# Low halves of the projection weights of tiles 3 to 7: GpSimd in the place of the vector engine

## The chip, the cores and the metric

The kernel runs on one core of a Trainium2 chip. The metric is the device time of one launch in microseconds (us). A core has five engines that run side by side, each with its own instruction queue: PE (TensorE, matrix products), DVE (the vector engine), ACT (ScalarE), POOL (GpSimd) and SP (SyncE, which here issues DMA transfers). SBUF is the on-chip memory that all of them read; PSUM is where PE puts its results.

## The reference

One layer of a decoder with 512 tokens and a model width of 1024. What matters here is the start: x is normalised, scaled and shifted by vectors that come from a condition c, and multiplied with a projection matrix. The rest (two groups of attention heads, gates, output projection) follows on its results.

```python
mod = jax.nn.silu(c) @ w_ada + b_ada
shift, scale, gate = jnp.split(mod, 3, axis=-1)
h = rms_norm(x, norm_gain) * (1 + scale[:, None, :]) + shift[:, None, :]
proj = h @ w_in
(q_a, k_a, v_a, z_a, q_b, kc, vc, ks, vs, kw, vw, z_b, g_b) = jnp.split(proj, _split_points(), axis=-1)
...
out = y.astype(x.dtype) @ w_out
return x + gate[:, None, :] * out
```

## The kernel before, in words

**Two halves for precision.** PE multiplies in a reduced float type, fp32r. To keep accuracy, every operand is split: the high half is the value copied into fp32r, the low half is the value minus its high half. A product of h and w is then three products: high h with high w, high h with low w, low h with high w.

**Phase one** makes the first 768 columns of the projection (q_a, k_a, v_a). The width of 1024 is cut into eight tiles of 128 rows, k = 0 to 7. For each tile:
- SP loads two transfers of rows of `w_ada` (`load_ada`, L232) and one piece of the projection weights, 128 x 768 (`load_wst`, L236). The staging tiles of both are rings of four (`ada_ring`, `wst_ring`), so the load for tile k + 4 waits for those who read tile k.
- DVE makes scale and shift of the tile with two row products over 1024 columns (`mod_rows`, L245; both inputs in SBUF), which leave one number per row in `AB`. For the first two tiles PE does this.
- DVE scales x by the norm (`scaled`, L296: `xT` from SBUF times `rbp` from PSUM).
- ACT makes `hh`, the high half of h, and `hf`, all of h (`h_high`, L302). DVE makes `hl`, the low half (`h_low`, L305; both inputs in SBUF).
- ACT makes the high half of the weights (`weights_high`, L288), and DVE the low half (`weights_low`, L291: `wst` minus the high half, both in SBUF). The halves lie in a ring of three pairs, named `sw0h`, `sw0l` to `sw2h`, `sw2l`; tile k uses pair k modulo 3.
- PE then runs `first_proj(k, n)` (L312, L313) for n = 0, 1, 2: high h with high w, high h with low w, low h with high w, each over four blocks of 128 tokens.

**The order** of this phase is written out by hand: all instructions are chained on each engine in the order in which they stand in the program (`in_order`). In the loop over k, `first_proj(k, 0)` and `first_proj(k, 1)` come first, then `new_tile(k + 1)`, then `first_proj(k, 2)`. `new_tile(k)` issues: `h_high(k)` on ACT; the first row product of tile k + 1 on DVE; `h_low(k)`; the second row product of tile k + 1; a scaling; the high half of the weights of tile k + 1 on ACT, and its low half on DVE. The scaling in it is that of tile k + 2 for k below 3, that of tile k + 1 for k from 4 to 6, and none for k = 3. So on DVE the low half of the weights of tile k + 1 is the last instruction of `new_tile(k)`, and the row products of the next `new_tile` stand behind it.

When phase one ends, ACT reads the sums from PSUM, and PE goes on with the next piece of the projection, whose weights are loaded through the `raw` tiles (`load_next`, L174) and split by `split` (ACT L192, DVE L193). GpSimd does little in the whole kernel: some memsets at the start, tiny copies of 128 x 2 in the attention (L1028), and a few transfers at the end.

Of the kernel before, what the change touches and what calls it, by code (L numbers as in the profile page):

```python
# [9 lines left out]
F32 = mybir.dt.float32  # L10
# [4 lines left out]
OP = mybir.AluOpType  # L15
# [18 lines left out]
NR = 4  # L34
LW = 4
PE_MODS = 2
GATE = {4: "kn2", 6: "qn11", 7: "qn11"}


# [36 lines left out]
@contextmanager  # L76
def in_order(tc, after=(), only=None):

    traced = tc.nc.cur_bb.bb.instructions
    n = len(traced)  # L80
    last = dict(after)
    yield last
    info = mybir.DependencyInfo(mybir.DependencyClass.NoSync, mybir.DependencyReason.DATA)
    for i in tc.nc.cur_bb.bb.instructions[n:]:
        if only and i.engine not in only:
            continue
        if i.engine in last:
            tc.add_manual_dep(i, last[i.engine].name, info, reason="in_order")
        last[i.engine] = i
# [3 lines left out]
def hybrid_layer_kernel(ctx, tc, A, out):  # L93
    nc = tc.nc
    PE, DVE, ACT, POOL, SP = nc.tensor, nc.vector, nc.scalar, nc.gpsimd, nc.sync
# [119 lines left out]
    ada, wst = {}, {}  # L215
# [5 lines left out]
    def load_ada(k):  # L221
        t = ada_ring[:, k % NR]
        if k < PE_MODS:
            ada[k] = t.rearrange("p (a b c) -> p a b c", a=8, b=2)
# [4 lines left out]
        else:  # L229
            ada[k] = t.rearrange("p (a b) -> p a b", a=2)  # L230
            for e in range(2):
                SP.dma_start(ada[k][:, e], A["w_ada_rows"][k - PE_MODS][:, e])  # L232

# [33 lines left out]
    hf, y, ws = {}, {}, {}  # L267
# [20 lines left out]
        ACT.activation(ws[k][0], wst[k], AF.Copy)  # L288

    def weights_low(k):  # L290
        DVE.tensor_tensor(ws[k][1], wst[k], ws[k][0].bitcast(F32), op=OP.subtract)  # L291

    def scaled(k, by, parts=(slice(0, S),)):
        y[k] = xT[k]
# [21 lines left out]
    with in_order(tc) as begun:  # L316
# [97 lines left out]
        ACT.copy(lsb[0:40, LINE - NEAR:LINE], pl)  # L414
        ACT.activation(hf[0], y[0], AF.Identity, bias=AB[:, 0, 1:2], scale=AB[:, 0, 0:1])
        weights_low(0)
        scaled(1, rbp)
        scaled(2, rbp)
# [3 lines left out]
        def new_tile(k):  # L422

            if k == 4:
                ACT.preload_act_table_set("exp_and_others")
            h_high(k, halves if k < 4 else (slice(0, S),))
            if k < 7:
                mod_rows(k + 1, (1 if k == 1 else 0,))
            h_low(k)
            if 1 < k < 7:  # L430
                mod_rows(k + 1, (1,))
            if k < 3:
                scaled(k + 2, rbp)
            if 4 <= k < 7:
                scaled(k + 1, rbp)
            if k < 7:
                weights_high(k + 1)
                weights_low(k + 1)

        for k in range(8):  # L440
            if k + NR < 8:
                load_ada(k + NR)
                load_wst(k + NR)
            elif k == LW:
                for _ in range(5):
                    load_next()
            first_proj(k, 0)
            if k == 0:
                mod_pe(1)
                weights_high(1)  # L450
                first_proj(0, 1, (0, 1))
                mod_col(1)
                mod_ab(1)
                weights_low(1)
                first_proj(0, 1, (2, 3))
            else:
                first_proj(k, 1)
            if k < 7:
                new_tile(k + 1)
            if k == 0:  # L460
                ACT.copy(lsb[0:8, LINE - NEAR - 128:LINE - NEAR], lsb[0:8, LINE - NEAR:LINE - NEAR + 128])
                ACT.copy(lsb[32:40, 0:LINE - NEAR], lsb[32:40, LINE - NEAR:LINE - NEAR + 1].to_broadcast([8, LINE - NEAR]))
                for a in range(2):
                    SP.dma_start(line_d[a], lsb[32 * a:32 * a + 8, :])
            if k >= 6:
                split_to("kv_cmp", 2 * (k - 6) + 1, 0)
            first_proj(k, 2)
# [291 lines left out]
    def gate_slice(q):  # L759

        for h in range(2):
            n, w = 2 * q + h, raws[f"gate{q}", h]
            with in_order(tc, {DVE.engine: marks[GATE[n]]} if n in GATE else {}, (DVE.engine,)):
                DVE.tensor_tensor_reduce(out=w, in0=w, in1=scrow, scale=0.5, scalar=prm[:, 16 + n:17 + n],
# [500 lines left out]
    with in_order(tc, last, (DVE.engine, ACT.engine)):  # L1265
# [3 lines left out]
        with in_order(tc, {PE.engine: last_pe()}, (PE.engine,)):  # L1269
            for name in TAIL.split():  # L1270
                op, rest = name[0], name[1:]
# [3 lines left out]
def _layout(inp):  # L1275
# [5 lines left out]
    halves = lambda t: cc(t.reshape(t.shape[0], 2, 4, t.shape[2]).transpose(1, 0, 2, 3))  # L1281
    wa = g("w_ada")[0].reshape(8, 128, 3, 8, 128)[:, :, 0:2, 0:PE_MODS]
    a["w_ada_cols"] = cc(wa.reshape(4, 2, 128, 2, PE_MODS, 128).transpose(4, 0, 2, 1, 3, 5).reshape(PE_MODS, 4, 128, 512))
    wr = g("w_ada")[0].reshape(D, 3, 8, 128)
    a["w_ada_rows"] = cc(wr[:, 0:2, PE_MODS:].transpose(2, 3, 1, 0))
    for q in range(4):
# [64 lines left out]
```

## Time and profile before

| | us |
|---|---|
| median of 3 runs | 299.51 |
| lowest and highest of these | 299.44, 300.15 |
| the profiled execution, its own time | 299.99 |
| its span in the trace | 297.7 |
| busy: PE, DVE, ACT, POOL | 290.1, 261.0, 205.1, 9.6 |
| first matmul of tile 3 and of tile 7 | 29.33, 46.99 |
| the low half of the weights on DVE (L291), one | 0.95 |

The span runs from the first to the last instruction in the trace; the time of the execution has some 2.3 us around it. Rows of a timeline show the start in us from the span's start, the length in us, the engine, the line, the operation, the tiles written and read, and in brackets how long the engine stood idle before it and what ended that. An instruction of DVE may start a little before the one in front of it has ended, so that the step from start to start is shorter than the length.

### The profile page before, as it was taken

To read this page: it belongs to the slowest core of one execution; us is meant where nothing else is said; L and a number is where in the kernel's file an instruction comes from. 1 tells how busy PE (TensorE), PEld (TensorE's weight loads), DVE (VectorE), ACT (ScalarE), POOL (GpSimd) and SP (SyncE) were. 2 spreads that over 40 slices of the span, in tenths; PEclk is the share of its full clock that TensorE was granted. 3 is DMA by queue.
4 is the path that set the end of the run, shared out by engine and by line. 5 is a ranking of instruction groups with operands and counts; after the bars stand their busy time and mean duration, and the time that the engine had idled before them with its cause. 6 is when DMAs were issued, how large, how long until landed. Compare 5 with 4: busy or idle time off the path is not lost.

```text
span 297.7 us, 6067 instructions
## 1 busy us (share of the span) xinstructions
PE 290.1 (97%) x2181; PEld 254.6 (86%) x2182; DVE 261.0 (88%) x730; ACT 205.1 (69%) x501; POOL 9.6 (3%) x28
## 2 busy tenths in 40 slices
PE   7999999999999999999999999999999999999995
PEld 3678888789989989989878988888888888889995
DVE  3689998999995998998999999999979779599992
ACT  5778657777848574967858567878877869567510
POOL 1000000000000100000000000000000000021210
PEclk9999999999999999999999999999999999999999
DMA  7999987842485884361402440223100120027272
GB/s 246 388 405 380 356 309 226 299 161 70 140 275 156 238 266 132 109 211 37 135 11 71 140 133 10 71 73 143 44 28 2 61 83 2 0 44 188 53 160 89
DMA packets 27417, 44.27 MB, mean 149 GB/s; under 512 B 1867, under 2 KB 18412, under 8 KB 27388
## 3 DMA queue, kind: packets, MB, share of 16 engines
q1 hardware_dynamic: 26380, 42.49, 42.2%
q0 software_dynamic: 864, 1.31, 3.0%
q8 instruction: 17, 0.28, 0.4%
q10 hardware_dynamic: 144, 0.09, 0.1%
q14 instruction: 12, 0.10, 0.1%
HBM read 41.74 MB, written 2.14 MB: 147 GB/s over the span
## 4 chain that ended last, share of the span: by engine, by line
PE 70%; DVE 13%; DMA 10%; ACT 3%; issue 2%; SPq 0%; DVEq 0%; ACTq 0%
PE pj L528 16%; PE pj L518 11%; PE po L1095 8%; PE pj L1205 6%; PE s L1004 5%; PE pt L1076 4%; DMA wst_ring<-in_w_qkv_a 4%; DMA ada_ring<-in_w_ada_rows 4%; PE s L1205 3%; PE pt L1062 3%; PE s L657 2%; DVE wl L193 2%; PE po L528 2%; DVE ada_ring L245 2%; PE s L1019 2%
## 5 line engine op out<-in xcount | busy, mean ns | idle before, releaser
L518 PE MATMUL pj<-wh,hh 128*128 128x256 f32 (+1 forms) x128 | 37.2, 291 | 0.0
L518 PE MATMUL pj<-wh,hl 128*128 128x256 f32 (+1 forms) x128 | 36.9, 288 | 0.0
L518 PE MATMUL pj<-wl,hh 128*128 128x256 f32 (+1 forms) x128 | 36.7, 287 | 0.0
L1010 ACT ACTIVATE pp<-pp,nm 128x256 f32<-128x256 f32 (+2 forms) x48 | 29.2, 610 | 6.3 <-DVE nm L1006 5.7
L528 PE MATMUL pj<-hh,wh 128*128 128x512 f32 x72 | 28.9, 402 | 0.0
L528 PE MATMUL pj<-hl,wh 128*128 128x512 f32 x72 | 28.8, 400 | 0.0
L528 PE MATMUL pj<-hh,wl 128*128 128x512 f32 x72 | 28.7, 399 | 0.0
L192 ACT ACTIVATE wh<-raw 128x512 fp32r<-128x512 f32 (+1 forms) x40 | 24.7, 635 | 5.3 <-PE pj L528 3.8
L193 DVE TENSOR_TENSOR wl<-raw,wh 128x512 fp32r<-128x512 f32 (+1 forms) x40 | 27.1, 692 | 1.4 <-ACT wh L192 1.1
L1006 DVE CUSTOM_DVE_ANT_0 pp<-s,bias 128x256 f32<-128x256 f32 (+2 forms) x48 | 25.5, 550 | 2.2 <-PE s L1004 2.0
L518 PEld LDWEIGHTS pj<-wh,hh 128*128 128x128 f32 x128 | 24.1, 189 | 0.4 <-issue 0.3
L518 PEld LDWEIGHTS pj<-wh,hl 128*128 128x128 f32 x128 | 24.2, 189 | 0.2 <-issue 0.2
L518 PEld LDWEIGHTS pj<-wl,hh 128*128 128x128 f32 x128 | 24.2, 189 | 0.1
L1004 PE MATMUL s<-kTb,qs 128*128 128x256 f32 (+2 forms) x96 | 23.6, 348 | 0.0
L1047 DVE TENSOR_SCALAR pp<-pp,rr,grev 128x256 f32<-128x256 f32 (+2 forms) x48 | 21.2, 474 | 0.3
L1004 PEld LDWEIGHTS s<-kTb,qs 128*128 128x128 f32 x96 | 16.9, 189 | 3.1 <-DVE nm L1006 0.3
L1010 ACT ACTIVATE pa<-pa,nm 128x129 f32<-128x129 f32 x32 | 12.7, 398 | 7.7 <-DVE nm L1026 6.0
L1077 ACT COPY ptT<-pt 128x384 f32<-128x384 f32 (+1 forms) x32 | 15.6, 526 | 1.1 <-PE pt L1076 1.0
L1063 ACT COPY ptT<-pt 128x256 f32<-128x256 f32 (+1 forms) x28 | 12.8, 457 | 4.1 <-PE pt L1062 3.7
L528 PEld LDWEIGHTS pj<-hh,wl 128*128 128x128 f32 x72 | 13.6, 188 | 2.4
L528 PEld LDWEIGHTS pj<-hl,wh 128*128 128x128 f32 x72 | 13.6, 189 | 2.3
L1076 PE MATMUL pt<-first,pp 128*128 128x128 f32 x112 | 15.5, 275 | 0.0
(320 smaller groups left out, 830.6 us busy)
## 6 DMA issues: line engine op xcount, KB each, us to landing
ada_ring<-in_w_ada_rows SPq DMA_DIRECT2D x12, 512.0 KB, 7.5
raw<-in_w_cmp SPq DMA_DIRECT2D x8, 512.0 KB, 6.6
raw<-in_w_gate SPq DMA_DIRECT2D x8, 512.0 KB, 4.5
raw<-in_w_o SPq DMA_DIRECT2D x8, 512.0 KB, 3.2
wst_ring<-in_w_qkv_a SPq DMA_DIRECT2D x8, 384.0 KB, 7.9
bias<-line_d SPq DMA_DIRECT2D x12, 256.0 KB, 4.0
xTp<-in_xT SPq DMA_DIRECT2D x8, 256.0 KB, 3.8
raw<-in_w_q_b SPq DMA_DIRECT2D x4, 512.0 KB, 4.8
```

What stands on the lines that cost most here:

```text
L192: ACT.activation(wh, src, AF.Copy)
L193: DVE.tensor_tensor(wl, src, wh.bitcast(F32), op=OP.subtract)
L518: PE.matmul(bank[:, t * n:(t + 1) * n], h[:, tb * 128:(tb + 1) * 128], w[:, k % 2, :], start=k == 0 and m == 0, stop=k == 7 and m == 2)
L528: PE.matmul(bank, w, h, start=k == 0 and m == 0, stop=k == 7 and m == 2)
L1004: PE.matmul(ps, qs[8 + 4 * g + r][:, 128 * i:128 * i + 128], kT[br, g][:, hl_, 0:w], start=hl_ == 0, stop=hl_ == 1)
L1006: DVE.tensor_tensor_reduce(out=P[:, g, 0:w], in0=ps, in1=bias["b", r, g][:, 512 - w:512], scale=1.0, scalar=3e38, op0=OP.add, op1=OP.min, ...
L1010: ACT.activation(P[:, g], P[:, g], AF.Exp, bias=nm[:, g:g + 1], scale=-1.0, accum_out=dn[:, g:g + 1])
L1047: DVE.tensor_scalar(v, v, rr[:, g:g + 1], gates[:, g, br:br + 1], op0=OP.mult, op1=OP.mult)
L1076: PE.transpose(pt[:, b * 128:(b + 1) * 128], P[:, g, b * 128:(b + 1) * 128], ident)
L1077: ACT.copy(T[:, 0:nb, :], rev(pt[:, 0:nb * 128].rearrange("p (b q) -> p b q", b=nb)))
L1095: PE.matmul(o[64 * g:64 * g + 64, 128 * i:128 * i + 128], vb[:, 64 * g:64 * g + 64], sl["T"][g][:, b, :], start=first_of and b == 0, stop= ...
L1205: PE.matmul(parts[g, p], a[:, r, :], b, start=new and r == 0 and m == 0, stop=r == 3 and m == 2, skip_group_check=True)
```

## The change

`weights_low` issues its subtraction on GpSimd for tiles 3 to 7 and on the vector engine for tiles 0 to 2. Operands, result, place in the program and the waits that follow from the data are the same. On GpSimd too the instructions of phase one are chained in program order.

```diff
 PE_MODS = 2
+POOL_LOWS = 3
 GATE = {4: "kn2", 6: "qn11", 7: "qn11"}
...
     def weights_low(k):
-        DVE.tensor_tensor(ws[k][1], wst[k], ws[k][0].bitcast(F32), op=OP.subtract)
+        (DVE if k < POOL_LOWS else POOL).tensor_tensor(ws[k][1], wst[k], ws[k][0].bitcast(F32), op=OP.subtract)
```

## The prediction

> **What bounds the kernel now.** I read the page's first part, then the stretches of the first phase by engine, then the timelines of DVE and ACT inside it. The page first:
>
> ```profile
> span 297.7 us, 6067 instructions
> PE 290.1 (97%) x2181; PEld 254.6 (86%) x2182; DVE 261.0 (88%) x730; ACT 205.1 (69%) x501; POOL 9.6 (3%) x28
> ```
>
> PE is busy for 290.1 of 297.7 us, so over the whole kernel it has 7.6 us idle: whatever makes PE late anywhere has little slack to vanish in later, and whatever makes it early can win little. GpSimd (POOL) is nearly empty. The change lies wholly in the first phase, the projection of eight weight tiles. This table has one row for each of tiles 2 to 6, from the first matmul of the tile to the first of the next (columns: stretch and its length, then busy time and instruction count of PE, PEld, DVE, ACT, POOL, then clock, DMA share, GB/s):
>
> ```profile
> 25.12:29.33 4.21, 4.21 (x26) 3.68 (x25) 3.85 (x8) 2.92 (x7) 0.00 (x0) 1.00 1.03 383
> 29.33:33.70 4.37, 4.37 (x27) 3.58 (x25) 4.37 (x7) 3.46 (x5) 0.00 (x0) 1.00 1.00 338
> 33.70:38.01 4.31, 4.31 (x26) 3.79 (x25) 4.16 (x8) 2.48 (x4) 0.00 (x0) 1.00 1.00 382
> 38.01:42.44 4.43, 4.37 (x26) 3.56 (x24) 4.43 (x8) 2.26 (x4) 0.00 (x0) 1.00 0.84 319
> 42.44:46.99 4.55, 4.46 (x25) 3.68 (x25) 4.45 (x7) 2.27 (x4) 0.00 (x0) 1.00 0.44 130
> ```
>
> Tile 2 takes 4.21 us with no gap: that is PE's own pace. The following four take 4.37, 4.31, 4.43 and 4.55, and DVE is full for nearly the whole of tiles 3, 5 and 6. So DVE limits this phase, but by little: from tile 4's start at 33.70, three tiles at PE's pace would bring tile 7 to 33.70 + 3 x 4.21 = 46.33 instead of 46.99. **0.66 us is all that freeing DVE can win here.** Why DVE is full, and how PE hangs on it, shows in the two timelines (start, length, engine, line):
>
> ```profile
> 32.07 0.96 DVE L291 TENSOR_TENSOR sw1l<-wst_ring,sw1h 128x768 fp32r<-128x768 f32 x1
> 32.94 1.28 DVE L245 CUSTOM_DVE_ANT_0 ada_ring<-ada_ring,scrow,first 128x1024 f32<-128x1024 f32 x1
> 34.14 0.09 DVE L245 DVE_READ_ACCUMULATOR2_ANT AB<- 128x1 f32 x1
> 34.38 0.69 DVE L305 TENSOR_TENSOR hl<-hf,hh 128x512 fp32r<-128x512 f32 x1 [0.15 <-ACT hf L302]
> 34.99 1.34 DVE L245 CUSTOM_DVE_ANT_0 ada_ring<-ada_ring,scrow,prmg 128x1024 f32<-128x1024 f32 x1
> 36.26 0.08 DVE L245 DVE_READ_ACCUMULATOR2_ANT AB<- 128x1 f32 x1
> 36.26 0.68 DVE L296 TENSOR_TENSOR xTp<-xTp,pj 128x512 f32<-128x512 f32 x1
> 36.86 0.95 DVE L291 TENSOR_TENSOR sw2l<-wst_ring,sw2h 128x768 fp32r<-128x768 f32 x1
> 37.73 1.28 DVE L245 CUSTOM_DVE_ANT_0 ada_ring<-ada_ring,scrow,first 128x1024 f32<-128x1024 f32 x1
> 38.93 0.08 DVE L245 DVE_READ_ACCUMULATOR2_ANT AB<- 128x1 f32 x1
> 38.93 0.68 DVE L305 TENSOR_TENSOR hl<-hf,hh 128x512 fp32r<-128x512 f32 x1
> 39.53 1.33 DVE L245 CUSTOM_DVE_ANT_0 ada_ring<-ada_ring,scrow,prmg 128x1024 f32<-128x1024 f32 x1
> 40.80 0.08 DVE L245 DVE_READ_ACCUMULATOR2_ANT AB<- 128x1 f32 x1
> 40.80 0.68 DVE L296 TENSOR_TENSOR xTp<-xTp,pj 128x512 f32<-128x512 f32 x1
> 41.40 0.95 DVE L291 TENSOR_TENSOR sw0l<-wst_ring,sw0h 128x768 fp32r<-128x768 f32 x1
> 42.27 1.28 DVE L245 CUSTOM_DVE_ANT_0 ada_ring<-ada_ring,scrow,first 128x1024 f32<-128x1024 f32 x1
> ...
> 45.34 0.68 DVE L296 TENSOR_TENSOR xTp<-xTp,pj 128x512 f32<-128x512 f32 x1
> ```
>
> ```profile
> 25.56 0.85 ACT L288 ACTIVATE sw0h<-wst_ring 128x768 fp32r<-128x768 f32 x1
> ...
> 39.77 0.85 ACT L288 ACTIVATE sw0h<-wst_ring 128x768 fp32r<-128x768 f32 x1 [1.22 <-DMA wst_ring<-in_w_qkv_a]
> ...
> 46.12 0.82 ACT L302 ACTIVATE hh<-xTp,AB 128x512 fp32r<-128x512 f32 x1 [2.28 <-DVE xTp L296]
> ```
>
> Per tile DVE does one row product (L245), the low half of h (L305), the second row product, the scaling of x (L296) and, last, the low half of the weights (L291), which the change moves. Starts follow each other faster than the lengths say, so I price by the step from one start to the next: low half of weights 0.87 (36.86 to 37.73), first row product 1.20, low half of h 0.60, second row product 1.27, scaling 0.60. The last scaling, at 45.34, releases ACT's high half hh at 46.12, and tile 7 starts on PE when that ends (46.12 + 0.82 = 46.94, start 46.99). So the scalings decide when tiles start, and the low half of the weights matters only as something that stands in front of the next scaling.
>
> **The change, part by part.** DVE loses five instructions, those of tiles 3 to 7, at 0.87 each: 4.35 us of DVE time. The one of tile 7 comes after the last scaling, so four can move a scaling. POOL gains the same five. No memory, transfer or order on the other engines changes.
>
> The price on POOL: the trace of before has no two-input instruction there. The nearest rows:
>
> ```profile
> 0.74 0.20 POOL L136 MEMSET ones_sq<- 128x128 f32 x1 [0.29 <-POOLq L1341]
> 0.88 0.41 POOL L321 MEMSET raw<- 8x384 f32 x1
> ```
>
> ```profile
> 98.81 0.65 POOL L1028 COPY pa<-nsink 128x2 f32<-128x2 f32 x1 [6.24 <-DVE csh L667]
> 101.39 0.19 POOL L1028 COPY pa<-nsink 128x2 f32<-128x2 f32 x1 [1.93 <-PE pt L1062]
> ```
>
> From 128 to 384 columns a memset grows by 0.21 us, 0.82 ns a column; one pass over 768 columns is 0.63. A tiny copy costs 0.19, which I take as the fixed part. If the two reads and the write run side by side, the instruction takes 0.19 + 0.63 = 0.82; if the two reads go in turn, 1.45; if the write goes in turn too, 2.08. DVE's 0.95 for the same shape shows no more than that 0.82 is fast. I take the middle of the two serial cases, **P = 1.76 us**, and keep 0.82 to 2.08. The Trainium skill (GPSIMD Engine Reference, section 3.1 Elementwise) gives 4497 ns for a two-input f32 add over 2048 columns; scaled to 768 columns that is an estimate of 1.69 us, no run here shows it, and the sum below would be +1.25 us by it.
>
> Whether POOL's work lies *beside* DVE's is the real question, and the copy of 0.65 us speaks to it. Beside it on DVE ran
>
> ```profile
> 98.74 0.68 DVE L571 TENSOR_TENSOR qn<-qraw,n_a 128x512 f32<-128x512 f32 x1
> ```
>
> with both inputs in SBUF. That instruction ended at 98.74 + 0.68 = 99.42, and the copy, begun at 98.81, ended at 99.46, 0.46 longer than the undisturbed one. I read this as a POOL read that could not go on until the two-input DVE instruction was through. The Trainium skill (SBUF — State Buffer, section Who interferes with whom) says that a DVE instruction with two SBUF inputs and a GpSimd instruction that reads SBUF contend for one read interface, and that the second to come is fully blocked; the trace agrees for a POOL copy behind DVE (0.65 against 0.19), and no row of before shows the other direction. On DVE the two row products and the low half of h have both inputs in SBUF; the scaling has one in PSUM (pj). I assume that the exclusion holds both ways and that POOL holds the interface for all of P. I also assume that POOL gets in only where DVE has no two-input instruction ready, since such instructions follow each other without a gap (the row product at 37.73 begins before 36.86 + 0.95 = 37.81).
>
> ```profile
> 27.52 0.68 DVE L296 TENSOR_TENSOR xTp<-xTp,pj 128x512 f32<-128x512 f32 x1
> 28.12 0.95 DVE L291 TENSOR_TENSOR sw0l<-wst_ring,sw0h 128x768 fp32r<-128x768 f32 x1
> 28.99 1.28 DVE L245 CUSTOM_DVE_ANT_0 ada_ring<-ada_ring,scrow,first 128x1024 f32<-128x1024 f32 x1
> ```
>
> The replay with P = 1.76, each DVE instruction at its step:
> - Tile 3's weights are ready at 25.56 + 0.85 = 26.41. POOL gets in beside the scaling, 27.52 to 29.28; the row product, free at 28.12, waits until 29.28 instead of starting at 28.99: **+0.29**, which is P - 0.60 - 0.87 (held, less the scaling beside it, less the instruction removed).
> - Tile 4: no scaling follows in that round. The row product of 32.94 now starts at 32.94 + 0.29 - 0.87 = 32.36 and ends at 33.57. DVE then must wait for ACT's hf (the row of 34.38), POOL gets in, and holds until 35.33. So the low half of h starts at 35.33 instead of 34.38: **+0.95**, with tile 3's 0.29 in it. The weights are late by 0.23 as well, since PE wants them a third into the tile, 33.70 + 1.40 = 35.10; that is covered, as tile 5 waits longer for its scaling.
> - Tiles 5 and 6: POOL beside the scalings, at 37.20 and 42.04, and the same +0.29 each. DVE is now behind its old times by 0.95 + 0.29 + 0.29 = **1.53**: the scaling of 45.34 comes at 46.87, hh at 47.65, and PE starts tile 7 at 48.52.
> - Tile 7's own low half runs from 46.87 to 48.63, before PE needs it at 48.52 + 1.40 = 49.92: nothing.
>
> In general the sum is 3(P - 1.47) + (P - 1.10) (three rounds beside a scaling, and tile 4's): +0.29 at P = 1.45, +1.53 at 1.76, +2.81 at 2.08. It crosses zero at 1.38 and 0.9 us at 1.60.
>
> What moves beside it costs nothing. The load of tile 7's weights goes into the staging slot of tile 3 and now waits for POOL until 29.28; SP's later loads wait in turn, for tile 5's low half and then for PE:
>
> ```profile
> SPq L174 <- DVE sw2l L291: 3.4, 1, 3.4
> SPq L174 <- PE skv L313: 3.2, 1, 3.2
> ```
>
> The 3.2 us wait for PE follows the one for DVE, so tile 5's low half may end later by up to 3.2 before that load notices; here it ends at 38.96 instead of 37.81. On POOL nothing stands behind the new instructions but the small copies of L1028 in the next phase. After tile 7 PE runs on, and with only 7.6 us of idle time in the whole span I carry the 1.53 to the end. The profiled execution took 299.99 us, 2.29 around its span of 297.7; it would become 301.5. It lies 0.48 above the median of 299.51, so on the median the forecast is 299.51 + 1.53 = **301.0 us**.
>
> **The rivals.**
> - *No exclusion.* The 0.65 us copy was late for another reason, and POOL works beside DVE. Then PE reaches its pace, up to 0.66 earlier; I take 0.6 of it, since some of tile 6's wait is for a transfer (the row of 39.77): 298.9. For: POOL is idle, and its instructions have a whole tile of time. Against: the copy's end 0.04 after the DVE instruction's end. It decides if L245 and L305 keep their lengths while POOL runs.
> - *Shared in turns.* The interface is taken read by read, so DVE loses only POOL's reads, 2 x 0.63 = 1.26 a round, 0.60 of it beside the scaling: less than the 0.87 removed. The sum with 1.26 in the place of P is 3 x (-0.21) + 0.16 = -0.47: 299.0. For: nothing in the trace. Against: the copy made no headway at all, small as it is.
> - *POOL gets in at every boundary.* If a waiting POOL comes before DVE's next instruction, one of its turns falls behind the low half of h, where no scaling covers it. At tile 6 that happens: its weights are ready at 39.77 + 0.85 = 40.62, just before the low half of h ends at 38.96 + 1.20 + 0.60 = 40.76. POOL holds to 42.52, and the second row product's 1.27 put the scaling at 43.79 instead of 40.80, tile 6 at 42.44 + 2.99 = 45.43 on PE, and tile 7, now at PE's own pace, at 49.64: **+2.65**, 302.2. For: a POOL that waits is there first. Against: DVE's instructions overlap, so there is no moment between two of them. It decides where POOL's turns begin, beside L296 or behind L305.
>
> **How the numbers follow.** The forecast 0.42, of which 0.10 at a P below 1.60, within 0.3% (0.9 us, about what a measurement of this kernel can tell from no change), and 0.32 slower. No exclusion 0.25: 0.22 within, 0.03 faster, since 0.66 is below 0.9. Shared 0.15: 0.11 within, 0.02 to each side. Every boundary 0.18, slower. So faster 0.05, same 0.43, slower 0.52. The forecast's own range, P from 1.45 to 2.08, is 299.8 to 302.3. The wide one reaches from no exclusion, 298.8, to every boundary with a P a little above mine, 302.8; beyond it lie every boundary with P near 2.08 and PE's full gain, some 0.15.
>
> **What would show it.** In the profile of after: five POOL instructions at L291 near 1.76 us, the first at 27.5; L245 or L305 starting late just when one ends, or lengthened by it; the scaling of 45.34 at about 46.9 and tile 7 on PE near 48.5. If POOL's instructions overlap unlengthened L245 rows, the exclusion is wrong and tile 7 starts near 46.4. If POOL takes over 2.1 us undisturbed, P is wrong and the time goes past 302.3.

## The result, and the profile after

| | before | after |
|---|---|---|
| median, us | 299.51 (7 runs, 299.22 to 300.15) | 302.4 (7 runs, 300.54 to 304.89) |
| ratio to before, with its 95% interval | | 1.0093 (1.0069 to 1.0117) |
| profiled execution and its span, us | 299.99, 297.7 | 302.68, 300.9 |

The changed kernel is slower by 2.9 us, 0.9%. The forecast was 301.0, slower, with a range from 298.8 to 302.8: the direction and the wide range hold, and the size is short by 1.4 us. The median lies just above the forecast's own range (299.8 to 302.3) and beside the rival "at every boundary" (302.2). The spread is new as well: 4.35 us from the lowest to the highest run, against less than 1 us before.

The page of the changed kernel first, its span and its busy times:

```profile
span 300.9 us, 6075 instructions
...
PE 289.7 (96%) x2182; PEld 254.3 (85%) x2182; DVE 262.9 (87%) x725; ACT 204.9 (68%) x501; POOL 22.1 (7%) x33
```

DVE has lost five instructions (730 to 725) and yet is busy for 1.9 us *more*. The stretches of tiles 2 to 6, each from the tile's first matmul to that of the next, show where (columns as in the prediction):

```profile
25.14:29.35 4.21, 4.21 (x26) 3.68 (x25) 4.00 (x7) 2.86 (x6) 2.86 (x1) 1.00 1.00 384
29.35:33.56 4.21, 4.21 (x26) 3.69 (x25) 4.09 (x6) 3.77 (x5) 2.62 (x1) 1.00 0.99 348
33.56:39.90 6.34, 4.38 (x26) 3.58 (x24) 6.34 (x7) 1.89 (x4) 2.10 (x2) 1.00 1.02 403
39.90:44.21 4.31, 4.31 (x25) 3.77 (x25) 3.87 (x7) 2.37 (x4) 2.84 (x1) 1.00 0.36 126
44.21:50.29 6.08, 4.38 (x26) 3.57 (x24) 5.12 (x6) 2.15 (x4) 2.10 (x2) 1.00 0.31 92
```

These five tiles take 25.15 us where they took 21.87, and 3.28 us is the whole loss: the span grew by 3.2. The time of this execution grew by less, 2.69 us (299.99 to 302.68), because the time around the span fell from 2.29 to 1.78. The same step shows in every run here: 2.2 to 2.4 us lie around the span where GpSimd has nothing to do in this phase (the kernel before and two of the variants below), 1.7 to 1.9 where it has. Why is not shown. A kernel with GpSimd work in this phase therefore gains some 0.5 us against the kernel before that do not come from the phase, and the span stands beside the time below where this matters. Two tiles carry it, the one that starts at 33.56 (6.34 us) and the one at 44.21 (6.08), while the tile before the first runs at PE's own 4.21. The timeline of GpSimd in this phase, and rows of DVE's, most of them around the first of the two tiles:

```profile
26.28 2.86 POOL L292 TENSOR_TENSOR sw0l<-wst_ring,sw0h 128x768 fp32r<-128x768 f32 x1 [24.98 <-ACT sw0h L289]
30.94 2.88 POOL L292 TENSOR_TENSOR sw1l<-wst_ring,sw1h 128x768 fp32r<-128x768 f32 x1 [1.80 <-ACT sw1h L289]
35.41 1.84 POOL L292 TENSOR_TENSOR sw2l<-wst_ring,sw2h 128x768 fp32r<-128x768 f32 x1 [1.59 <-ACT sw2h L289]
41.37 2.87 POOL L292 TENSOR_TENSOR sw0l<-wst_ring,sw0h 128x768 fp32r<-128x768 f32 x1 [4.12 <-ACT sw0h L289]
45.58 2.06 POOL L292 TENSOR_TENSOR sw1l<-wst_ring,sw1h 128x768 fp32r<-128x768 f32 x1 [1.33 <-ACT sw1h L289]
```

```profile
27.97 2.26 DVE L246 CUSTOM_DVE_ANT_0 ada_ring<-ada_ring,scrow,first 128x1024 f32<-128x1024 f32 x1
...
32.23 2.67 DVE L246 CUSTOM_DVE_ANT_0 ada_ring<-ada_ring,scrow,first 128x1024 f32<-128x1024 f32 x1
...
34.83 0.68 DVE L306 TENSOR_TENSOR hl<-hf,hh 128x512 fp32r<-128x512 f32 x1
35.43 2.90 DVE L246 CUSTOM_DVE_ANT_0 ada_ring<-ada_ring,scrow,prmg 128x1024 f32<-128x1024 f32 x1
38.26 0.08 DVE L246 DVE_READ_ACCUMULATOR2_ANT AB<- 128x1 f32 x1
38.26 0.68 DVE L297 TENSOR_TENSOR xTp<-xTp,pj 128x512 f32<-128x512 f32 x1
38.86 1.27 DVE L246 CUSTOM_DVE_ANT_0 ada_ring<-ada_ring,scrow,first 128x1024 f32<-128x1024 f32 x1
40.07 0.07 DVE L246 DVE_READ_ACCUMULATOR2_ANT AB<- 128x1 f32 x1
40.59 0.69 DVE L306 TENSOR_TENSOR hl<-hf,hh 128x512 fp32r<-128x512 f32 x1 [0.44 <-ACT hf L303]
41.20 1.34 DVE L246 CUSTOM_DVE_ANT_0 ada_ring<-ada_ring,scrow,prmg 128x1024 f32<-128x1024 f32 x1
...
42.46 0.68 DVE L297 TENSOR_TENSOR xTp<-xTp,pj 128x512 f32<-128x512 f32 x1
43.06 2.27 DVE L246 CUSTOM_DVE_ANT_0 ada_ring<-ada_ring,scrow,first 128x1024 f32<-128x1024 f32 x1
...
45.86 2.86 DVE L246 CUSTOM_DVE_ANT_0 ada_ring<-ada_ring,scrow,prmg 128x1024 f32<-128x1024 f32 x1
```

Two things are to be seen. A row product that meets GpSimd is not shown as late but as *long*: 2.90 instead of 1.34 where GpSimd got in just behind the low half of h, 2.27 instead of 1.27 where it got in beside the scaling. And GpSimd's own lengths vary in the same way: 2.86, 2.88 and 2.87 are subtractions that had to wait for a row product before them; the third, at 35.41, started at once and took 1.84. It was there 0.02 us before the row product of 35.43.

### The profile page after: what moved, and what is told of

Read it like the earlier page. It is cut to its first block, busy times and chain, and to the rows that moved or that the text cites. A ratio compares the mean times of both kernels' runs of the same rounds, so it can differ in the third digit from the quotient of the medians.

```text
span 300.9 us, 6075 instructions
## 1 busy us (share of the span) xinstructions
PE 289.7 (96%) x2182; PEld 254.3 (85%) x2182; DVE 262.9 (87%) x725; ACT 204.9 (68%) x501; POOL 22.1 (7%) x33
## 3 DMA queue, kind: packets, MB, share of 16 engines
HBM read 41.74 MB, written 2.14 MB: 146 GB/s over the span
## 4 chain that ended last, share of the span: by engine, by line
PE 70%; DVE 14%; DMA 11%; issue 2%; ACT 2%; SPq 0%; ACTq 0%; DVEq 0%
PE pj L529 16%; PE pj L519 11%; PE po L1096 8%; PE pj L1206 6%; PE s L1005 5%; DMA ada_ring<-in_w_ada_rows 5%; PE pt L1077 4%; DVE ada_ring L246 4%; PE s L1206 3%; PE pt L1063 3%; PE s L658 2%; DVE wl L194 2%; DMA rest<-in_rest 2%; DMA ada_ring<-in_w_ada_cols 2%; PE po L529 2%
```

## The experiments

Theory: a vector-engine instruction with two SBUF inputs and a GpSimd instruction that reads SBUF shut each other out for a whole instruction, and who asks first goes first. The rivals stand in each expectation. Times are medians, and each ratio is to the kernel before as it ran beside that experiment: 299.58 us with a span of 297.3 for the memsets, the copy, the row sums and the kernel without the subtractions, 299.74 us with a span of 297.4 for the other four.

**Which kind of GpSimd work holds the vector engine.** The kernel before, with memsets added:

```diff
 def weights_low(k):
     DVE.tensor_tensor(ws[k][1], wst[k], ws[k][0].bitcast(F32), op=OP.subtract)
+    if k >= 3:
+        POOL.memset(hf[k - 1][:, 0:8], 0.0)
+        for m in range(3):
+            POOL.memset(scr, 0.0)
```

> The kernel before, with three more GpSimd memsets of 128x768 into a scratch tile for each of tiles 3 to 7, placed to run while the vector engine does its row products; they write and read nothing. Theory (the vector engine's instructions with two SBUF inputs are shut out by GpSimd's READS, through one read interface): the row products keep 1.28 and 1.34 us, tile 7 starts on PE within 0.15 us of 46.99, and the time is that of before, 299.5 (within 0.3%). Rival (any GpSimd instruction that uses SBUF holds the vector engine): row products grow to over 2 us, and some 2.1 us of memset in each of four rounds, less 0.6 beside a scaling, cost over 4 us: above 303.5.

299.22 us, ratio 0.9984 (0.9974 to 0.9994). The timelines of GpSimd and of DVE in one round:

```profile
39.87 2.35 POOL L296 MEMSET scr<- 128x768 f32 x3
```

```profile
39.69 1.34 DVE L245 CUSTOM_DVE_ANT_0 ada_ring<-ada_ring,scrow,prmg 128x1024 f32<-128x1024 f32 x1
...
41.55 0.96 DVE L292 TENSOR_TENSOR sw0l<-wst_ring,sw0h 128x768 fp32r<-128x768 f32 x1
```

2.35 us of memsets, from 39.87 to 42.22, lie over a row product and a subtraction, both with two SBUF inputs, and neither is longer than before. These writes do not hold DVE. The 0.36 us below the kernel before are no gain of this phase: the span is 297.45 against 297.3, and the difference is the time around it. Next, one read stream instead of two, again in the kernel before:

```diff
 def weights_low(k):
     DVE.tensor_tensor(ws[k][1], wst[k], ws[k][0].bitcast(F32), op=OP.subtract)
+    if k >= 3:
+        POOL.tensor_copy(scr, ws[k][0].bitcast(F32))
```

> The kernel before, with one more GpSimd copy of 128x768 for each of tiles 3 to 7, from the high half of the weights into a scratch tile: one read stream instead of the two of the subtraction. Theory (held for as long as GpSimd reads): one instruction of 128x768 on the vector engine that starts behind the copy's start is lengthened in each round by about half of what the subtraction cost, 0.6 to 0.9 us where nothing covers it and 0 to 0.3 beside a scaling; tile 7 starts on PE 0.5 to 3 us later than 46.99 and the time is 300 to 302.5. Rival (only a GpSimd instruction with two inputs contends): all lengths on the vector engine as before, 299.5.

301.43 us, ratio 1.0048 (1.0028 to 1.0068). GpSimd and DVE in the same round:

```profile
40.37 0.88 POOL L294 COPY scr<-sw0h 128x768 f32<-128x768 f32 x1 [4.17 <-ACT sw0h L289]
```

```profile
40.49 1.84 DVE L245 CUSTOM_DVE_ANT_0 ada_ring<-ada_ring,scrow,prmg 128x1024 f32<-128x1024 f32 x1
```

The copy takes 0.88, and the row product behind it grows by 0.50, from 1.34 to 1.84; so do those of tiles 5 and 7, and the subtraction in tile 4's round, the next two-input instruction there, grows by 0.61. The one beside a scaling cost 0.02 (the subtraction behind it took 0.97 instead of 0.95). One input suffices on GpSimd's side; the hold is a third of the subtraction's 1.56, and in three of the rounds below the 0.6 that I had named as the least.

**Which instructions of the vector engine are held.** In the changed kernel, row products became row sums:

```diff
 def mod_rows(k, es=(0, 1)):
     for e in es:
+        if k >= 4:
+            DVE.tensor_reduce(AB[:, k, 1 - e:2 - e], ada[k][:, e], AX.X, OP.add)
+            continue
```

> The changed kernel, with the row products of tiles 4 to 7 replaced by a plain sum along the row (a reduce of the same 1024 columns with one SBUF input; the product with the condition's row, its factor and its start value are left out, so scale and shift are not the reference's). Theory (only instructions with two SBUF inputs are held): the reduces take one and the same length each, near 1.2 us, whether GpSimd runs beside them or not; only the low half of h can still be held; tile 7 starts on PE before 47.0 and the time is at most 299.5. Rival (GpSimd slows whatever the vector engine does, by sharing SBUF or in some other way): the reduces beside GpSimd grow to 2.2 to 2.9 us as the row products did, and the time stays near 302.4.

298.88 us, ratio 0.9985 (0.9967 to 1.0003), 3.5 us below the change; one of the ten runs took 301.25, which no profile explains. GpSimd's subtraction of one round and DVE beside it:

```profile
34.89 1.86 POOL L295 TENSOR_TENSOR sw2l<-wst_ring,sw2h 128x768 fp32r<-128x768 f32 x1 [1.92 <-ACT sw2h L292]
```

```profile
34.52 1.22 DVE L247 TENSOR_REDUCE AB<-ada_ring 128x1 f32<-128x1024 f32 x1
35.65 0.68 DVE L300 TENSOR_TENSOR xTp<-xTp,pj 128x512 f32<-128x512 f32 x1
36.36 1.22 DVE L247 TENSOR_REDUCE AB<-ada_ring 128x1 f32<-128x1024 f32 x1
```

The sums take 1.22 whether GpSimd runs beside them or not, and the subtraction starts in the middle of one and still takes 1.86, so GpSimd does not wait either. A sum also writes almost nothing, so this run by itself could speak of the row product's output; but the scaling writes 512 columns to SBUF, with its second input in PSUM, and is 0.68 beside GpSimd's reads in every trace. The subtraction that the copy lengthened by 0.61 writes to SBUF as the scaling does and differs from it in its second input, which lies in SBUF. What is left is the second SBUF input. The control is the same replacement in the kernel before:

> The control of the run with one-input row sums: the kernel before, with the same replacement for tiles 4 to 7 (the product with the condition's row, its factor and its start value are left out), all low halves on the vector engine. Theory: the reduces take what they take there with GpSimd beside them, to 0.05 us, and the kernel is within 0.3% of the one with GpSimd or up to 0.7 us slower, since the vector engine has 0.87 us more to do per tile. Rival: with nothing on GpSimd the reduces are clearly shorter.

299.07 us, ratio 0.9971 (0.9961 to 0.9981); the sums take 1.21 and 1.22. The two times can't tell more, since in both kernels tiles 2 to 6 take 21.07 us (46.12 - 25.05 and 46.27 - 25.20), which is PE's own pace; it is the lengths of the sums that agree.

**How much there was to win.** The kernel before without the five subtractions:

```diff
 def weights_low(k):
+    if k >= 3:
+        return
     DVE.tensor_tensor(ws[k][1], wst[k], ws[k][0].bitcast(F32), op=OP.subtract)
```

> The kernel before, with the low halves of the weights of tiles 3 to 7 left out on every engine (PE multiplies with what lies in the ring). This is what the change would be worth if GpSimd's part were free. Theory (PE's own pace is the next bound): tile 7 starts on PE at 46.3 to 46.5 instead of 46.99, and the time falls by 0.5 to 0.7 us, to 298.9. Rival (the vector engine's 4.35 us come back in full): 295.2.

299.12 us, ratio 0.9984 (0.9975 to 0.9994). Tiles 2 to 6 take 46.64 - 25.57 = 21.07 us, five times PE's 4.21, against 21.87. So 0.80 us of this phase is all that a free GpSimd could give, less than a fifth of the 4.35 us of DVE time; in the median 0.46 us of it are seen (0.45 in the span, 296.85 against 297.3).

**Who goes first.** Only the subtraction of tile 7 on GpSimd, where DVE has nothing to win:

```diff
-POOL_LOWS = 3
+POOL_LOWS = 7
```

> Only the subtraction of tile 7 on GpSimd, those of tiles 0 to 6 on the vector engine. It is the last one and stands behind the last scaling, so the vector engine gains nothing by it. Theory (first to ask gets the interface): GpSimd asks some 0.05 us after ACT's high half of tile 7 ends, 43.9 in the profile of before, while the low half of h (43.47 to 44.07) runs, gets in behind it, and holds the second row product by about 1.5 us: tile 7 starts on PE 1.3 to 1.6 us later, 300.8 to 301.2. Rival (GpSimd only gets in where the vector engine has a gap, as I forecast): it runs beside the last scaling, and the time is that of before.

301.27 us, ratio 1.0046 (1.0029 to 1.0063), for one instruction. GpSimd and DVE:

```profile
43.88 1.84 POOL L292 TENSOR_TENSOR sw1l<-wst_ring,sw1h 128x768 fp32r<-128x768 f32 x1 [42.59 <-ACT sw1h L289]
```

```profile
43.29 0.69 DVE L306 TENSOR_TENSOR hl<-hf,hh 128x512 fp32r<-128x512 f32 x1
43.90 2.90 DVE L246 CUSTOM_DVE_ANT_0 ada_ring<-ada_ring,scrow,prmg 128x1024 f32<-128x1024 f32 x1
```

DVE had the row product ready and no gap, and GpSimd got in all the same, 0.02 us ahead: 1.56 us more, and tile 7 starts on PE at 48.37 instead of 46.99. The rival here was my forecast's own rule, and it falls. One of the seven runs took 299.81; that fits a round in which DVE was first, but no trace of that run exists. The reverse experiment keeps GpSimd back in the changed kernel until the low half of h is through, so that it asks during the second row product and gets in beside the scaling:

```diff
 def weights_low(k):
+    if k >= POOL_LOWS and k != 4:
+        POOL.memset(hf[k - 1][:, 0:1], 0.0)
     (DVE if k < POOL_LOWS else POOL).tensor_tensor(ws[k][1], wst[k], ws[k][0].bitcast(F32), op=OP.subtract)
```

> The changed kernel, with GpSimd's subtractions of tiles 3, 5, 6 and 7 kept back (by a tiny memset that waits until the low half of h of the tile before has been read) so that they ask for the read interface while the second row product runs, and so get it beside the scaling. Tile 4's, which has no scaling behind it, is as in the change. Theory (the interface goes to who asks first, for about 1.6 us, and only what lies beside a one-input instruction is free): the two row products that were lengthened by some 1.55 us behind a low half of h (tile 5 and tile 7) are no longer, the ones behind a scaling grow by some 1.0; tile 7 starts on PE about 1.1 us earlier than in the change, near 49.2, and the time is 301.0 to 301.6, with a smaller spread than the change's 300.5 to 304.9. Rival (the moment of asking does not matter): as the change, 302.4, spread alike.

301.06 us (five runs, 300.7 to 301.69), ratio 1.0045 (1.0033 to 1.0057). GpSimd and DVE in one round:

```profile
36.26 2.81 POOL L294 TENSOR_TENSOR sw2l<-wst_ring,sw2h 128x768 fp32r<-128x768 f32 x1
```

```profile
37.29 0.68 DVE L299 TENSOR_TENSOR xTp<-xTp,pj 128x512 f32<-128x512 f32 x1
37.89 2.27 DVE L246 CUSTOM_DVE_ANT_0 ada_ring<-ada_ring,scrow,first 128x1024 f32<-128x1024 f32 x1
```

The three row products behind a scaling take 2.27, 2.27 and 2.25, the one in tile 4's round, left as it was, 2.89, and all others 1.27 to 1.34. The spread is 1 us. Tile 7 starts at 48.25, not 49.2: I had counted 0.58 for moving its subtraction from an uncovered place to a covered one, but behind the *last* scaling nothing waits, and the whole 1.56 goes (1.56 + 0.58 = 2.14, measured 50.29 - 48.25 = 2.04). Not all of this reaches the end: from tile 7's start to the end of the span it is 251.55 us here and 250.61 in the profile after, so 0.94 is lost again behind phase one; where and why was not followed.

Three more profiles of the changed kernel ask whether the moment of asking also makes the spread:

> The changed kernel once more, one look, because its runs spread from 300.54 to 304.89 us where those of before stay within 1 us. Theory (who asks first gets the read interface, so a few hundredths of a us decide whether a subtraction gets in behind the low half of h, at 1.56 us, or beside a scaling, at 0.98): the number of row products lengthened by some 1.55 differs from look to look, and the time follows the sum of the lengthenings, to 0.3 us. Rival (the spread comes from elsewhere, say the transfers): the same rows are lengthened by the same amounts and the time differs all the same.

> The same kernel, another look on the same chip: as for the one before it. Theory: time differences between looks equal the differences in the summed lengthenings of the row products and low halves of h of phase one, to 0.3 us. Rival: they don't.

> The same kernel, a third look on the same chip, with the same expectations of both theories.

They took 301.04, 301.52 and 301.49 us beside a kernel before of 299.51. In the first of them GpSimd asks at tile 5 at 35.41, as in the profile after, but DVE is 0.25 us earlier, and the order turns round:

```profile
35.41 2.81 POOL L292 TENSOR_TENSOR sw2l<-wst_ring,sw2h 128x768 fp32r<-128x768 f32 x1 [1.84 <-ACT sw2h L289]
```

```profile
35.18 1.33 DVE L246 CUSTOM_DVE_ANT_0 ada_ring<-ada_ring,scrow,prmg 128x1024 f32<-128x1024 f32 x1
36.45 0.08 DVE L246 DVE_READ_ACCUMULATOR2_ANT AB<- 128x1 f32 x1
36.45 0.68 DVE L297 TENSOR_TENSOR xTp<-xTp,pj 128x512 f32<-128x512 f32 x1
37.05 2.25 DVE L246 CUSTOM_DVE_ANT_0 ada_ring<-ada_ring,scrow,first 128x1024 f32<-128x1024 f32 x1
```

The row product of 35.18 keeps its 1.33, GpSimd waits (2.81 instead of 1.84) and gets in beside the scaling, at 0.98 to the next row product. So the same kernel takes different places from run to run, as expected. The amounts were expected to agree to 0.3 us, and they do not: the lengthenings of the row products sum to 6.47 in the profile after, then 5.04, 5.93 and 5.85. The second and third of the new ones agree in both. From the first to the second it is 0.89 by the sum and 0.48 in time, and from the second to the profile after 0.54 by the sum and 1.16 in time. What the sum leaves out is DVE's own waits between tile 4's scaling and tile 7's: 0.71 in the profile after, then 0.57, 0.14 and 0.24. About half a us of the first two is a wait for ACT's hf behind an uncovered hold (the row of 40.59 above; one at tile 6 in the other). With the waits the sums are 7.18, 5.61, 6.07 and 6.09, and their differences, 0.46 and 1.11, are those of the time. So in these four profiles the spread arises here, on DVE, but the lengthenings alone do not give it. Why a run goes up to 304.89 stays open: no profile shows one.

**A version that beats both.** From this the subtraction has to be short enough for the scaling to cover it. The kernel before, with a third of the columns on GpSimd in the three rounds that have a scaling in front of another row product:

```diff
 def weights_low(k):
+    if k in (3, 5, 6):
+        POOL.memset(hf[k - 1][:, 0:1], 0.0)
+        for e, c in ((DVE, slice(0, 512)), (POOL, slice(512, 768))):
+            e.tensor_tensor(ws[k][1][:, c], wst[k][:, c], ws[k][0].bitcast(F32)[:, c], op=OP.subtract)
+        return
     DVE.tensor_tensor(ws[k][1], wst[k], ws[k][0].bitcast(F32), op=OP.subtract)
```

> The kernel before, with the last 256 of the 768 columns of the low halves of tiles 3, 5 and 6 on GpSimd, kept back in the same way so that they run beside the scaling; the other 512 columns, and tiles 4 and 7 whole, stay on the vector engine. Theory (GpSimd holds the interface for some 2 ns a column and a fixed part, here 0.5 to 0.7 us, the scaling beside it takes 0.60, and the vector engine saves 0.27 a tile): tile 7 starts on PE 0.3 to 0.66 us earlier than 46.99, the time is 298.9 to 299.3. Rival (any two-input work on GpSimd costs the vector engine more than it saves): 299.6 or more.

298.77 us, ratio 0.9970 (0.9961 to 0.9980): 0.9 us less than before and 3.6 less than the change. Of the 0.9, only 0.4 are in the span (297.0 against 297.4); the rest is the time around it. GpSimd's second part, then DVE beside it:

```profile
35.15 1.59 POOL L294 TENSOR_TENSOR sw2l<-wst_ring,sw2h 128x256 fp32r<-128x256 f32 x1
```

```profile
36.07 0.68 DVE L301 TENSOR_TENSOR xTp<-xTp,pj 128x512 f32<-128x512 f32 x1
36.67 0.68 DVE L294 TENSOR_TENSOR sw2l<-wst_ring,sw2h 128x512 fp32r<-128x512 f32 x1
37.27 1.28 DVE L245 CUSTOM_DVE_ANT_0 ada_ring<-ada_ring,scrow,first 128x1024 f32<-128x1024 f32 x1
```

GpSimd waits for the row product and is through at 36.74, 0.67 us after the scaling's start; nothing on DVE is longer than before. Tiles 2 to 6 take 46.51 - 25.44 = 21.07: PE's pace again, as in the kernel without the five subtractions. That one has a ratio of 0.9984, but wins as much in its span, 0.45 us: what sets the two apart is the time around the span.

## Why the prediction was right in kind and short in size

- **PE's pace as the limit of the gain: right, a little narrow.** I had 0.66 from tile 4 on; 0.80 was there, because the 0.16 that tile 3 took above PE's pace (4.37) also went.
- **The price of one subtraction: right as a number, in part by luck.** 1.76 was forecast between bounds of 0.82 and 2.08; undisturbed it takes 1.84 to 1.86 (rows of 35.41 above, of 34.89 with row sums). But 1.76 was the middle between two cases. The copy, with one read and one write, takes 0.88, little more than a memset of the same shape (2.34 for three): by these numbers its write does not come in turn. That speaks for the case of 1.45, in which a second read adds 0.63; measured it adds 0.96 (1.84 - 0.88).
- **The exclusion both ways: right, and shown.** GpSimd behind DVE: 2.86 to 2.88. DVE behind GpSimd, which no row of before had: 2.26 to 2.90. The Trainium skill (SBUF — State Buffer, section Who interferes with whom) says that such a DVE instruction contends with a GpSimd instruction that reads and not with one that only writes, and the runs agree: copies lengthened it by 0.50 to 0.61, memsets by nothing.
- **The hold beside a scaling: a little too dear.** P - 0.60 gives 1.16; measured 0.98. I had GpSimd hold for all of P; the row product's extra time ends 0.26 before GpSimd does (35.43 + 1.56 = 36.99 against 35.41 + 1.84 = 37.25), so that without cover it is 1.56.
- **Where GpSimd gets in: wrong, and this is the step that failed.** I assumed that it enters "only where DVE has no two-input instruction ready", because DVE's instructions overlap. The profile after, and the run with tile 7 alone, show it entering between two such instructions whenever it asked first. In the profile after, tiles 4, 5 and 7 were uncovered: 1.40, 1.56 and 1.52, where I had one. This was the rival "at every boundary", though it struck at tiles 5 and 7 and not at tile 6, where I had put it; in one of the later profiles tile 6 was struck. What this step cost can be read off: the kernel that keeps GpSimd back has nearly the places that I had assumed (three beside a scaling, tile 4's uncovered), and there tile 7's scaling follows tile 4's after 46.61 - 27.47 = 19.14 us, 1.32 more than before, where 1.53 was forecast. In the change it comes 3.47 later than before, so the places cost the other 2.15.
- **The sum.** From tile 4's scaling to tile 7's, DVE's five row products are longer by 6.47 and four subtractions of 0.87 are gone: +2.99. DVE's waits went from 0.24 (for hf) to 0.71 (0.52 for hf, as hh comes after the late scaling, and 0.19 in front of a row product): +0.47. Together 3.46; measured (48.66 - 27.37) - (45.34 - 27.52) = 3.47. Forecast 1.53.
- **Carried to the end: right in the span, wrong around it.** 3.3 us at tile 7's start, 3.2 in the span, but 2.69 in the time. I had taken the 2.29 around the span over unchanged; it is 1.78. That the median lies inside the wide range is owed to this: with 0.51 more it would be near 302.9, and the range ended at 302.8.

## What to carry to other kernels

Moving an elementwise operation with two SBUF inputs from a full vector engine to an idle GpSimd was no free move here: for most of the time that GpSimd's instruction took, the row products and the subtraction, the vector instructions with two SBUF inputs that it met, stood still. So what counts is how much one-input or PSUM work lies beside it. Cut the piece to the length of that work and time it with a dependency; left to chance, it goes in wherever it asks first, and the time spreads. Ask first what the freed engine can bring: here 4.35 us of vector time were worth 0.8 in the phase. And compare spans as well as times: where a kernel gave GpSimd work in this phase, 0.5 us of the difference lay outside the span.

## What was not expected of the hardware

- The held time is recorded as the length of the waiting instruction, on both engines (DVE 2.90 for 1.34, GpSimd 2.88 for 1.84), so DVE's busy time rose although it had less to do.
- A lead of 0.02 us was enough: GpSimd's instruction starts at 43.88, DVE's at 43.90, and DVE's is 1.56 us longer.
- The hold ends before GpSimd's instruction does, by the same 0.26 us for a copy (40.49 + 0.50 = 40.99 against 41.25) and for a subtraction (36.99 against 37.25). What GpSimd does in that time is not shown.
- With work for GpSimd in phase one, memsets included, the time around the span is 0.5 us shorter (1.7 to 1.9 against 2.2 to 2.4). The cause stays open.
